# A layer's opening: the first tile's modulation weights, scale ahead of shift, and a small vector on another queue

## The chip, the cores and the metric

The kernel runs on one core of one Trainium2 chip. The metric is the device time of one execution in microseconds. A core has five engines that run side by side and are kept in step by semaphores: TensorE (PE in the profile) for matrix products, with its weight loads shown apart as PEld, VectorE (DVE), ScalarE (ACT), GpSimd (POOL) and SyncE (SP), which here does little else than issue DMA transfers. [...]

## The reference, cut to what matters

One layer over 512 latent tokens and 256 context tokens of 1024 channels. Before the first norm is used, a vector `c` (and `c_ctx` for the context) is turned into a scale and a shift for each channel:

```
mod = silu(c) @ w_mod + b_mod                # 6 x 1024 values; the same for c_ctx
sh1, sc1, gt1, sh2, sc2, gt2 = split(mod, 6)
h = rmsnorm(x, norm1_g) * (1 + sc1) + sh1    # latent; the context with its own sc1, sh1
p = h @ w_in                                 # one wide projection; its column groups feed two mixers
...
o  = merge(ssd mixer, window attention, two sigmoid gates) @ w_out
x  = x + gt1 * o
x  = x + gt2 * conv_ffn(rmsnorm(x, norm2_g) * (1 + sc2) + sh2)
return rmsnorm(x, final_g)
```

All of this is in float32. The kernel holds a float32 operand as a high part and a low part and forms a product from three matrix products: high by high, high by low, low by high.

## The kernel before, in words

Channels lie on the 128 partitions, so 1024 channels are eight tiles, j = 0 to 7, and tokens run along the free axis. The change touches only the opening stage, up to about 62 us, in which the norm's scales and shifts are computed while the first five column blocks of the projection (the gates, `w0`, 640 columns) and then one q and one k block are multiplied.

The projection does not wait for the norm's root. For tiles j = 0 to 4 the kernel multiplies `x * a1` (a1 is the channel's `(1 + scale) * norm gain`), multiplies the sums by the root later (`sc`), and adds the part that comes from the shifts as a bias, which is formed from products of the shifts with `w0` (`Z`). For tiles 5 to 7 the whole normed value is used. So per tile j the steps are, by the names that the plan gives them:

- `Lm(2j)`, `Lm(2j+1)`: two loads of modulation weights, 512 KB each (`load_mod`, L433 to L435). `Lx`: a tile of x, 256 KB. `Lw`: a tile of `w0`, 320 KB. `Lv`, once: the vectors (`vec`) and the identity (`ident`).
- `A(j).0`, `A(j).1` on PE (`mod_rows`, L474 to L479): each load holds four of the eight blocks of input channels, for 256 output columns, 128 of shift and 128 of scale. Both are needed before any value is complete. Four products go to four strips of 32 rows of the accumulator `pmod`.
- `tm(j)` on ACT (`mod_copy`, L483) copies the sums out; `B(j)` on PE (`mod_cols`, L487) adds the four strips and turns the row into a column, once for the shift and once for the scale, with a small matrix `sel2` that `tv` (`tables`, L402 to L405, DVE) makes from `ident`; `a(j)` on DVE (`mod_put`, L490 and L491) writes `a1` and `s1`.
- `hi(j)` (ACT, L503) and `lo(j)` (DVE, L507): the high and the low part of `x * a1`. `wh(j)` (ACT, L495) and `wl(j)` (DVE, L499): those of `w0`.
- `P(j).i.t` on PE (`product`, L523): for five column blocks i the three products t = 0, 1, 2 (wh with hi, wh with lo, wl with hi), 15 for a tile.
- `s(j)` (DVE, L622) and `Z(j)` on PE (`shifts`, L542): the products of the shifts with `w0`.
- `sq(j)`, `ad(j)`, and once `S`, `m`, `R`, `T`, `p`: sums of squares, root and its spread. `n(j)` and what follows: the normed value with its high and low parts.

Before the plan, `cc` (the two vectors `c`, 8 KB) is loaded into `ccs` by a DMA that ACT issues (L386). ACT and DVE turn it into silu values, laid out in `csil32` as weights of 32 columns (L393 to L397). Nine warm-ups (`warm`, L407 to L409, a product of ones with ones that nobody reads) keep PE busy meanwhile. A float32 product shows as two PE records.

The order on PE, ACT and DVE in this stage is written out at build time by a planner (`Plan`, L282 to L357). Each step, an "atom", has an engine, a cost, the steps that it needs and a rank. The planner walks through simulated time, takes for each engine the lowest rank that is ready (or the one that is ready first), and emits the steps in that order inside a `manual_schedule` block. SP's loads keep the order in which they are listed; their time comes from bytes over a common bus. The starting points are given at the call:

```
run_plan(first_.order({"ACT": 3.0, "DVE": 3.6, "SP": 0.7}, bus=2.76))
```

More warm-ups are atoms too: two after A0.0, two after A0.1, five after B0 (L601 to L603). Outside such blocks the order within an engine comes from the framework; at a few places `keep_in_program_order` binds it.

Of the kernel before, what the change touches and what calls it, by code (L numbers as in the profile page):

```python
# [13 lines left out]
ALU = mybir.AluOpType  # L14
# [4 lines left out]
P = 128  # L19
# [3 lines left out]
KT = D // P  # L23
# [4 lines left out]
V_BMOD = 0  # L28
# [16 lines left out]
def tile_hybrid_layer(  # L45
# [30 lines left out]
    nc = tc.nc  # L76
    V, S, G, T = nc.vector, nc.scalar, nc.gpsimd, nc.tensor
# [123 lines left out]
    ccs = cpool.tile([P, KT, 2], F32, name="ccs")  # L201
# [10 lines left out]
    s1 = cpool.tile([P, KT, 2], F32, name="s1")  # L212
# [11 lines left out]
    def col(base, i):  # L224
        return vec[:, base + i : base + i + 1]
# [151 lines left out]
    with tc.tile_pool(name="spool", bufs=1) as sp:  # L377
# [5 lines left out]
        sel4 = sp.tile([P, 4], F32, name="sel4")  # L383
        gb = cpool.tile([P, 8], F32, name="gb")

        S.dma_start(ccs, cc)  # L386
        G.memset(csil32, 0.0)
        G.memset(s32, 0.0)
        G.memset(phalf, -0.5)
# [19 lines left out]
            T.matmul(pg[NG - 1][:, 0:P], ones, ones, start=True, stop=True, skip_group_check=True)  # L409
# [23 lines left out]
        def load_mod(i):  # L433
            t = mod_raw[i] = sp.tile([P, 4, 256], F32, tag="wm", name="wm", bufs=6)
            nc.sync.dma_start(t, wm1[i].rearrange("p (k c) -> p k c", k=4))  # L435

        def load_w0(j):
            r = w0_raw[j] = sp.tile([P, 640], F32, tag="w0", name="w0", bufs=4)
            nc.sync.dma_start(r, w0[j])
# [17 lines left out]
            nc.sync.dma_start(ident, ident_d)  # L457

        for j in range(KT):
            for i in (2 * j, 2 * j + 1):  # L460
                load_atom("Lm%d" % i, 512, lambda i=i: load_mod(i), ["A%d.%d" % divmod(i - 6, 2)] if i > 5 else [])
# [12 lines left out]
        def mod_rows(j, u):  # L474

            w = mod_raw.pop(2 * j + u)
            for k in range(4):
                z = slice(32 * k, 32 * k + 32)
                T.matmul(pmod[z, 0:256], csil32[:, 4 * u + k, :], w[:, k, :], start=u == 0, stop=u == 1)  # L479

        def mod_copy(j):
            rows[j] = tmp("tm")[:, :256]
            S.copy(rows[j], pmod[:, 0:256])  # L483

        def mod_cols(j):
            for i in range(2):
                T.matmul(pmod[:, 256 + 2 * i : 258 + 2 * i], rows[j][:, i * P : (i + 1) * P], sel2, start=True, stop=True)  # L487

        def mod_put(j):
            V.tensor_scalar(a1[:, j, :], pmod[:, 258:260], bp1[:, j : j + 1], col(V_N1, j), ALU.add, ALU.mult)  # L490
# [28 lines left out]
        def part(ps, key, n, w, h, t):  # L519

            a, b = ((0, 0), (0, 1), (1, 0))[t]
            c = B_[key] = B_.get(key, 0) + 1
            T.matmul(ps, w[a], h[b], start=c == 1, stop=c % n == 0, skip_group_check=True)  # L523

        def product(j, i, t):
            h = (hi_[j], lo_[j]) if j < NU else (hlh[:, j, :], hll[:, j, :])

            n = 3 * NU if j < NU else 3 * KT
            part(pg[i], ("P", i), n, [w[j][:, i * P : (i + 1) * P] for w in (wh, wl)], h, t)

        def product2(n, k, t):

# [65 lines left out]
            V.tensor_scalar_mul(nsink, bcs[:, 32:48], -1.0)  # L598

        CR = 450  # L600
        for x, n in (("A0.0", 2), ("A0.1", 2), ("B0", 5)):  # L601
            for i in range(n):
                atom("W%s.%d" % (x, i), "PE", 0.23, [x], 0, warm)  # L603
        r = {}
        cq = tmp("te")[:, :LC]
        for j in range(KT):
            R, js = 100 * j, "%d" % j
            for u in range(2):
                needs = ["Lm%d" % (2 * j + u)] + (["A%d.0" % j] if u else ["tm%d" % (j - 1)] if j else [])
                atom("A%d.%d" % (j, u), "PE", 0.5, needs, R - 110 + u, lambda j=j, u=u: mod_rows(j, u))  # L610
            needs = ["A%d.1" % j] + (["B%d" % (j - 1)] if j else [])
            atom("tm" + js, "ACT", 0.37, needs, R - 108, lambda j=j: mod_copy(j))
            needs = ["tm" + js, "a%d" % (j - 1) if j else "tv"]
            atom("B" + js, "PE", 0.4, needs, R - 107, lambda j=j: mod_cols(j))
            atom("a" + js, "DVE", 0.41, ["B" + js], R - 106, lambda j=j: mod_put(j))
            old = ["P%d.%d.%d" % (j - 2, i, t) for i in range(NG) for t in range(3)] if j > 1 else []
            atom("wh" + js, "ACT", 0.72, ["Lw" + js] + old, R - 60, lambda j=j: w_high(j))
            atom("wl" + js, "DVE", 0.82, ["wh" + js] + ["a0"] * (j == 0), R - 60, lambda j=j: w_low(j))
            if j < NU:
                atom("hi" + js, "ACT", 0.72, ["a" + js, "Lx" + js] + old, R - 100, lambda j=j: x_high(j))  # L620
                atom("lo" + js, "DVE", 0.75, ["hi" + js] + old, R - 100, lambda j=j: x_low(j))
                atom("s" + js, "DVE", 0.15, ["a" + js], R - 70, lambda j=j: V.tensor_copy(s32[:, j, 0:1], s1[:, j, 0:1]))  # L622
# [1289 lines left out]
def pack(  # L1912
# [71 lines left out]
```

## Time and profile before

| | us |
|---|---|
| median of three runs | 1260.78 |
| the runs | 1264.44, 1260.48, 1260.78 |
| the profiled execution's own time | 1263.37 |
| its span, first to last instruction | 1261.6 |

The mean granted clock of TensorE in the profiled execution is 0.995 of full speed. In the profile, an L number is a line of the kernel. A row of the timeline gives start, length, engine, line, operation, out<-in, how many instructions were merged, and in brackets how long the engine had been idle before and what released it. The chain is the sequence of work that ended last, followed back from the last instruction. A DMA row gives the size and the time from issue to landing, the waiting in its queue included. Names of tiles stand without their numbers: `wm` are the modulation weights, `w` the tiles of `w0`, `ah` and `al` are hi and lo, `mis` the accumulators of the five column blocks, `acc` holds `pmod` and the bias sums.

### The profile page before, as it was taken

The page shows a single profiled execution, that of the slowest core. Times are in us where ns is not written, and L with a number is a line of the kernel's source. Part 1 is how long each engine was busy: PE and PEld are TensorE (multiplying, and loading weights), DVE is VectorE, ACT ScalarE, POOL GpSimd, SP SyncE. Part 2 cuts the span into 40 slices and gives each one's busy share as a digit, 9 for nine tenths or more (in the row PEclk, how much of TensorE's full clock was granted, in tenths as well). Part 3 has the DMA queues.
Part 4 walks back from the last instruction along what each step waited for, and adds up shares of the span by engine and source line. Part 5 has one row for each costly group of instructions (what it writes and reads, how often), then busy time and mean ns, then how long its engine had stood idle before and what let it go on. Part 6 is the DMA issues. An engine that isn't in the chain of part 4 may idle for free.

```text
span 1261.6 us, 17339 instructions
## 1 busy us (share of the span) xinstructions
PE 1245.1 (99%) x6466; PEld 1029.8 (82%) x6466; DVE 878.7 (70%) x1417; ACT 656.3 (52%) x1223; POOL 138.5 (11%) x113
## 2 busy tenths in 40 slices
PE   9999999999999999999999999999999999999997
PEld 6798888888788788787787787889988888888886
DVE  4857788888636688878988667676777777773333
ACT  4658788887344476565565653223544444442221
POOL 0000000000000143343343420000200000000000
PEclk9999999999999999999999999999999999999998
DMA  9652143212354235445347378775233333333331
GB/s 375 232 135 91 56 134 91 92 61 78 133 166 130 89 107 157 133 125 181 101 124 219 109 244 268 240 245 196 73 112 117 117 114 105 116 113 92 103 94 67
DMA packets 90996, 174.57 MB, mean 138 GB/s; under 512 B 7712, under 2 KB 43360, under 8 KB 90912
## 3 DMA queue, kind: packets, MB, share of 16 engines
q1 hardware_dynamic: 89680, 172.40, 42.9%
q8 instruction: 51, 0.84, 0.3%
q10 hardware_dynamic: 1232, 1.06, 0.2%
q14 instruction: 33, 0.27, 0.1%
HBM read 150.82 MB, written 17.11 MB: 133 GB/s over the span
## 4 chain that ended last, share of the span: by engine, by line
PE 83%; DVE 8%; ACT 2%; DMA 2%; POOL 2%; issue 1%; DVEq 0%; SPq 0%; POOLq 0%; ACTq 0%
PE acc L191 19%; PE acc L194 19%; PE acc L192 19%; PE score L884 3%; PE po L933 3%; PE mis L523 2%; PE pt L920 2%; DVE wlo L149 2%; PE mis L1507 1%; PE mis L1501 1%; PE acc L1003 1%; PE acc L1005 1%; PE acc L1004 1%; PE acc L1794 1%; PE acc L1664 1%
## 5 line engine op out<-in xcount | busy, mean ns | idle before, releaser
L149 DVE TENSOR_TENSOR wlo<-wraw,whi 128x1024 fp32r<-128x1024 f32 (+1 forms) x128 | 163.9, 1281 | 119.0 <-ACT whi L148 118.0
L148 ACT CAST whi<-wraw 128x1024 fp32r<-128x1024 f32 (+1 forms) x128 | 132.1, 1033 | 179.1 <-PE acc L192 122.8
L191 PE MATMUL acc<-hlh,whi 128*128 128x512 f32 x472 | 193.9, 411 | 0.0
L194 PE MATMUL acc<-hlh,wlo 128*128 128x512 f32 x472 | 185.1, 392 | 0.0
L192 PE MATMUL acc<-hll,whi 128*128 128x512 f32 x472 | 184.5, 391 | 0.0
L191 PE MATMUL acc<-mh,whi 128*128 128x512 f32 x368 | 143.4, 390 | 0.0
L192 PE MATMUL acc<-ml,whi 128*128 128x512 f32 x368 | 143.2, 389 | 0.0
L194 PE MATMUL acc<-mh,wlo 128*128 128x512 f32 x368 | 143.2, 389 | 0.0
L194 PEld LDWEIGHTS acc<-hlh,wlo 128*128 128x128 f32 x472 | 88.6, 188 | 19.6
L192 PEld LDWEIGHTS acc<-hll,whi 128*128 128x128 f32 x472 | 88.9, 188 | 17.5 <-issue 2.4
L191 PEld LDWEIGHTS acc<-hlh,whi 128*128 128x128 f32 x472 | 88.8, 188 | 17.0 <-issue 2.4
L194 PEld LDWEIGHTS acc<-mh,wlo 128*128 128x128 f32 x368 | 69.1, 188 | 14.4
L191 PEld LDWEIGHTS acc<-mh,whi 128*128 128x128 f32 x368 | 69.1, 188 | 14.4
L192 PEld LDWEIGHTS acc<-ml,whi 128*128 128x128 f32 x368 | 69.1, 188 | 14.2
L1415 POOL TENSOR_TENSOR st<-st,eT 128x512 f32<-128x512 f32 x24 | 29.4, 1224 | 409.0 <-ACT st L1432 389.5
L893 DVE CUSTOM_DVE_ANT_0 p<-score,winm,nsink 128x512 f32<-128x512 f32 (+1 forms) x64 | 51.9, 811 | 16.4 <-PE score L884 14.9
L191 PE MATMUL acc<-fh,whi 128*128 128x512 f32 x154 | 60.0, 390 | 0.0
L194 PE MATMUL acc<-fh,wlo 128*128 128x512 f32 x154 | 59.9, 389 | 0.0
L192 PE MATMUL acc<-fl,whi 128*128 128x512 f32 x154 | 59.9, 389 | 0.0
L245 POOL TENSOR_TENSOR rs<-ms,phalf 128x2 f32<-128x2 f32 (+1 forms) x5 | 4.8, 951 | 490.6 <-DVE ms L244 490.6
L900 ACT ACTIVATE p<-p,mneg 128x512 f32<-128x512 f32 (+1 forms) x64 | 49.7, 777 | 16.1 <-DVE mneg L893 15.6
L1314 ACT ACTIVATE ta<-acc,half 128x512 f32<-128x512 f32 (+1 forms) x66 | 46.6, 706 | 20.1 <-PE acc L194 18.9
(365 smaller groups left out, 2917.9 us busy)
## 6 DMA issues: line engine op xcount, KB each, us to landing
wraw<-wup SPq DMA_DIRECT2D x44, 512.0 KB, 3.5
fb<-cs_d SPq DMA_DIRECT2D x32, 512.0 KB, 5.8
wraw<-wm SPq DMA_DIRECT2D x32, 512.0 KB, 3.8
wraw<-wx SPq DMA_DIRECT2D x24, 512.0 KB, 3.5
wm<-wm SPq DMA_DIRECT2D x16, 512.0 KB, 8.1
wraw<-wz SPq DMA_DIRECT2D x16, 512.0 KB, 3.6
wraw<-wos SPq DMA_DIRECT2D x16, 512.0 KB, 4.9
wraw<-wdn SPq DMA_DIRECT2D x16, 512.0 KB, 3.4
```

The source lines that it names most:

```text
L148: S.copy(hi[:, :n], r[:, :n])
L149: V.tensor_tensor(lo[:, :n], r[:, :n], raw(hi[:, :n]), ALU.subtract)
L191: T.matmul(ps, wh, xh[:, k0 + k, :], start=a, stop=False)
L192: T.matmul(ps, wh, xl[:, k0 + k, :], start=False, stop=False)
L194: T.matmul(ps, wl, xh[:, k0 + k, :], start=False, stop=b)
L523: T.matmul(ps, w[a], h[b], start=c == 1, stop=c % n == 0, skip_group_check=True)
L884: T.matmul(ps[:, o : o + len(z) * P], Q[h][:, b * P : (b + 1) * P], k[:, j, z[0] * P : (z[-1] + 1) * P], start=v == 0 and o % 512 in (0, P ...
L893: V.tensor_tensor_reduce(p[:, :w], d["ps"][i][:, o0 : o0 + w], m, op0=ALU.add, op1=ALU.min, scale=1.0, scalar=nsink[:, h : h + 1], accum_o ...
L900: S.activation(p, p, AF.Exp, bias=d["mneg"][:, i : i + 1], scale=-1.0, accum_out=d["den"][:, i : i + 1])
L933: T.matmul(d["po"], vst[:, cols[x], j, :], d[y][x], start=x == 0 and y == "pth", stop=x == c - 1 and y == "ptl")
L1314: S.activation(o[:, :n], ps[:, :n], AF.Identity, scale=hcol(base_w, stride + i), bias=hcol(base_b, i))
L1415: G.tensor_tensor(h8(n), h8(s), bc64(eT[:, z0 : z0 + 8, c]), ALU.mult)
```

## The change

For the first tile (j = 0) only, the two modulation loads no longer hold four blocks of input channels each for shift and scale together. Lm0 holds all eight blocks for the 128 scale columns, Lm1 all eight for the 128 shift columns; the arrays are laid out so on the host. Lm0 stays at the head of the loads, Lm1 moves behind the first tile of `w0`. A0.0, A0.1, tm0 and B0 become two chains: A0a, tma, B0a for the scale, which `a0` needs, and A0b, tmb, B0b for the shift, which `s0` needs. A0b waits for the tile's first product P0.0.0, tmb for B0a. The shift's two DVE operations become the step `s0`. Lm6 and Lm7, which reuse the two buffers, wait for A0a and A0b.

The load of `cc` goes from ACT's queue to SP's, ahead of all other loads. The opening warm-ups become ten; the warm-ups in the plan are two after A0a and six after B0a. `wl1` now needs `a1`, `B1` needs `s0`, and the norm of a tile needs its shift. The planner's starting points are changed.

```diff
-        S.dma_start(ccs, cc)
+        nc.sync.dma_start(ccs, cc)
...
-            for _ in range(9):
+            for _ in range(10):
                 warm()
...
         for j in range(KT):
-            for i in (2 * j, 2 * j + 1):
+            for i in (2 * j, 2 * j + 1)[: 1 + (j > 0)]:
...
             load_atom("Lw%d" % j, 320, lambda j=j: load_w0(j), old)
+            if j == 0:
+                load_atom("Lm1", 512, lambda: load_mod(1))
...
+        def mod_first(u):
+            w = mod_raw.pop(u).rearrange("p k (a c) -> p (k a) c", a=2)
+            for k in range(KT):
+                z = slice(32 * (k % 4), 32 * (k % 4) + 32)
+                T.matmul(pmod[z, P - P * u : 2 * P - P * u], csil32[:, k, :], w[:, k, :], start=k < 4, stop=k > 3)
+
+        def first_copy(u):
+            rows[u, 0] = tmp("tm")[:, :P]
+            S.copy(rows[u, 0], pmod[:, P - P * u : 2 * P - P * u])
+
+        def first_cols(u):
+            T.matmul(pmod[:, 258 - 2 * u : 260 - 2 * u], rows[u, 0], sel2, start=True, stop=True)
+
+        def first_shift():
+            V.tensor_scalar(s1[:, 0, :], pmod[:, 256:258], col(V_BMOD, 0), None, ALU.add)
+            V.tensor_copy(s32[:, 0, 0:1], s1[:, 0, 0:1])
...
-            V.tensor_scalar(s1[:, j, :], pmod[:, 256:258], col(V_BMOD, j), None, ALU.add)
+            if j:
+                V.tensor_scalar(s1[:, j, :], pmod[:, 256:258], col(V_BMOD, j), None, ALU.add)
...
-        for x, n in (("A0.0", 2), ("A0.1", 2), ("B0", 5)):
+        for x, n in (("A0a", 2), ("B0a", 6)):
             for i in range(n):
-                atom("W%s.%d" % (x, i), "PE", 0.23, [x], 0, warm)
+                atom("W%s.%d" % (x, i), "PE", 0.23, [x], -1, warm)
...
+            if j == 0:
+                for u, x in enumerate("ab"):
+                    atom("A0" + x, "PE", 0.55, ["Lm%d" % u] + ["P0.0.0"] * u, R - 110 + 40 * u, lambda u=u: mod_first(u))
+                    atom("tm" + x, "ACT", 0.25, ["A0" + x] + ["B0a"] * u, R - 108 + 40 * u, lambda u=u: first_copy(u))
+                    atom("B0" + x, "PE", 0.25, ["tm" + x, "tv"], R - 107 + 40 * u, lambda u=u: first_cols(u))
...
-            atom("wl" + js, "DVE", 0.82, ["wh" + js] + ["a0"] * (j == 0), R - 60, lambda j=j: w_low(j))
+            atom("wl" + js, "DVE", 0.82, ["wh" + js] + ["a" + js] * (j < 2), R - 60, lambda j=j: w_low(j))
...
+                    atom("s0", "DVE", 0.3, ["B0b"], R - 70, first_shift)
...
-            needs = ["pl", "a" + js, "sq" + js] + (["lo" + js] if j < NU else [])
+            needs = ["pl", "a" + js, "sq" + js] + (["lo" + js, "s" + js] if j < NU else [])
...
-        run_plan(first_.order({"ACT": 3.0, "DVE": 3.6, "SP": 0.7}, bus=2.76))
+        run_plan(first_.order({"PE": 5.2, "ACT": 3.0, "DVE": 3.6, "SP": 1.2}, bus=3.2))
...
+    m0 = w_mod[:, :2048].reshape(KT, P, 2, KT, P)[:, :, ::-1, 0, :]
+    d["wm1"][0:2] = m0.transpose(2, 1, 0, 3).reshape(2, P, 1024)
```

More of the change, by code (lines that the diff above doesn't have):

```diff
@@ L459, in tile_hybrid_layer @@
         for j in range(KT):
-            for i in (2 * j, 2 * j + 1):
-                load_atom("Lm%d" % i, 512, lambda i=i: load_mod(i), ["A%d.%d" % divmod(i - 6, 2)] if i > 5 else [])
+            for i in (2 * j, 2 * j + 1)[: 1 + (j > 0)]:
+                load_atom("Lm%d" % i, 512, lambda i=i: load_mod(i), ["A%d.%d" % divmod(i - 6, 2) if i > 7 else ("A0a", "A0b")[i - 6]] if i > 5 else [])
             if j == 0:
@@ L525, in product @@
         def product(j, i, t):
-            h = (hi_[j], lo_[j]) if j < NU else (hlh[:, j, :], hll[:, j, :])
+            h = (hi_.get(j), lo_.get(j)) if j < NU else (hlh[:, j, :], hll[:, j, :])
             n = 3 * NU if j < NU else 3 * KT
-            part(pg[i], ("P", i), n, [w[j][:, i * P : (i + 1) * P] for w in (wh, wl)], h, t)
+            part(pg[i], ("P", i), n, [w[j][:, i * P : (i + 1) * P] if j in w else None for w in (wh, wl)], h, t)
         def product2(n, k, t):
@@ L607, in tile_hybrid_layer @@
             R, js = 100 * j, "%d" % j
-            for u in range(2):
-                needs = ["Lm%d" % (2 * j + u)] + (["A%d.0" % j] if u else ["tm%d" % (j - 1)] if j else [])
-                atom("A%d.%d" % (j, u), "PE", 0.5, needs, R - 110 + u, lambda j=j, u=u: mod_rows(j, u))
[L611 to L615, printed above, removed]
+            if j == 0:
[3 more added lines that the diff above has]
+                    atom("B0" + x, "PE", 0.25, ["tm" + x, "tv"], R - 107 + 40 * u, lambda u=u: first_cols(u))
+            for u in range(2 if j else 0):
+                needs = ["Lm%d" % (2 * j + u)] + (["A%d.0" % j] if u else ["tm%d" % (j - 1) if j > 1 else "tmb"])
+                atom("A%d.%d" % (j, u), "PE", 0.5, needs, R - 110 + u, lambda j=j, u=u: mod_rows(j, u))
+            if j:
+                needs = ["A%d.1" % j] + (["B%d" % (j - 1)] if j > 1 else [])
+                atom("tm" + js, "ACT", 0.37, needs, R - 108, lambda j=j: mod_copy(j))
+                needs = ["tm" + js, "a%d" % (j - 1)] + ["s0"] * (j == 1)
+                atom("B" + js, "PE", 0.4, needs, R - 107, lambda j=j: mod_cols(j))
+            atom("a" + js, "DVE", 0.41 if j else 0.25, ["B" + js] if j else ["B0a"], R - 106, lambda j=j: mod_put(j))
             old = ["P%d.%d.%d" % (j - 2, i, t) for i in range(NG) for t in range(3)] if j > 1 else []
             atom("wh" + js, "ACT", 0.72, ["Lw" + js] + old, R - 60, lambda j=j: w_high(j))
-            atom("wl" + js, "DVE", 0.82, ["wh" + js] + ["a0"] * (j == 0), R - 60, lambda j=j: w_low(j))
+            atom("wl" + js, "DVE", 0.82, ["wh" + js] + ["a" + js] * (j < 2), R - 60, lambda j=j: w_low(j))
             if j < NU:
```

5 lines of the change are left out of this document (4 added, 1 removed).

## The prediction

> **What bounds the kernel now.** I read the page first, then the chain that ended last, cut to the opening, then the opening's timeline and its DMA issues, and last a table of stages. The page:
>
> ```profile
> span 1261.6 us, 17339 instructions
> PE 1245.1 (99%) x6466; PEld 1029.8 (82%) x6466; DVE 878.7 (70%) x1417; ACT 656.3 (52%) x1223; POOL 138.5 (11%) x113
> ```
>
> TensorE (PE) is busy for 99% of the span, so a saving in the opening lasts to the end if it lets PE begin *useful* work sooner and PE then stays fed. PE's warm-up products (L409) count as busy too, so the opening has to be read by name. The pieces of the chain that ended last (start, length, what):
>
> ```profile
> 0.73 4.15 DMA ccs<-cc
> ...
> 5.64 0.19 DVE csil L397
> 5.87 0.64 PE acc L479 x8
> ...
> 7.15 0.57 PE acc L479 x8
> 8.82 1.22 PE mis L409 x10
> 10.04 0.24 PE acc L542
> 12.17 0.57 PE acc L479 x8
> 14.10 0.34 PE acc L487 x4
> 24.54 0.56 PE acc L542 x4
> ```
>
> The conditioning vector `ccs` lands at 4.88 us, ScalarE (ACT) and VectorE (DVE) turn it into `csil32` by 5.83, and only then does the first modulation product A0.0 start, at 5.87. Until 10.04 PE alternates between first-tile products and warm-ups; a warm-up is time that PE had nothing to do. The same opening on the timeline (start, length, engine, line, what):
>
> ```profile
> 1.05 3.73 PE L409 MATMUL mis<-ones 128*128 128x128 f32 x18 [1.05 <-DVE ones L392]
> 2.12 0.43 SPq L457 DMA_DIRECT2D ident<-ident_d  x1
> 2.59 0.71 SPq L442 DMA_DIRECT2D xsb<-xT  x1
> 3.34 0.43 SPq L439 DMA_DIRECT2D w<-w  x1
> 6.88 0.16 DVE L405 TENSOR_SCALAR bp<-vec 128x8 f32<-128x8 f32 x1
> 7.79 0.37 ACT L483 COPY tm<-acc 128x256 f32<-128x256 f32 x1 [2.67 <-PE acc L479]
> 8.15 0.72 ACT L495 CAST w0h<-w 128x640 fp32r<-128x640 f32 x1
> 8.21 0.61 PE L487 MATMUL acc<-sel,tm 128*128 128x2 f32 x4
> 8.92 0.28 DVE L490 TENSOR_SCALAR a<-acc,bp,vec 128x2 f32<-128x2 f32 x1 [1.88 <-ACT w0h L495]
> 9.23 0.72 ACT L503 ACTIVATE ah<-xsb,a 128x512 fp32r<-128x512 f32 x1 [0.35 <-DVE a L490]
> 9.86 0.61 ACT L549 ACTIVATE ssq<-xsb 128x512 f32<-128x512 f32 x1
> 9.97 0.41 PE L542 MATMUL acc<-w,s 128*32 128x256 f32 x3
> 10.96 0.50 PE L523 MATMUL mis<-ah,w0h 128*128 128x512 f32 x1
> ```
>
> From 9.97 us PE does only useful work: Z0 and A1.0 woven together (9.97 to 10.96), then the first tile's products P0. That point, 9.97, is what the change has to beat. And two rows of the stage table (length, then busy time of each engine, granted clock, DMA share, GB/s):
>
> ```profile
> 10.00:40.00 30.00, 30.00 (x216) 19.82 (x216) 17.89 (x41) 16.48 (x34) 1.47 (x1) 1.00 1.03 411
> 40.00:62.00 22.00, 22.00 (x128) 17.01 (x127) 21.37 (x42) 13.99 (x27) 1.61 (x1) 1.00 0.50 176
> ```
>
> PE is without a gap in both stretches; DMA is full to 40 us, DVE nearly full (21.37 of 22) behind it. PE ends last, with two neighbours close by.
>
> **The change, part by part.** Landings come from the DMA issues of the first 5 us (KB each, then median us from issue to landing), one row for the first `wm` load alone, and small stores from the whole run:
>
> ```profile
> wm<-wm SPq DMA_DIRECT2D x4, 512.0 KB, 5.2
> ident<-ident_d SPq DMA_DIRECT2D x1, 64.0 KB, 4.6
> xsb<-xT SPq DMA_DIRECT2D x1, 256.0 KB, 4.7
> w<-w SPq DMA_DIRECT2D x1, 320.0 KB, 4.8
> ccs<-cc ACTq DMA_DIRECT2D x1, 8.0 KB, 4.2
> ```
> ```profile
> DMA to landing us min/median/max: 4.0/4.0/4.0
> ```
> ```profile
> tt_d<-tt SPq DMA_DIRECT2D x2, 0.4 KB, 2.7
> tt_d<-tt SPq DMA_DIRECT2D x2, 0.1 KB, 1.9
> ```
>
> *1. `cc` goes first on SP's queue.* It moves from ACT's queue, where it was issued at 0.73, to SP's, ahead of every other load. Every SP load is therefore issued one slot later; the slot is about 0.45 us (from `ident` at 2.12 to `xsb` at 2.59 is 0.47). For `cc` nothing stands in front any more. Its landing is bounded from below by the small stores (1.9 and 2.7 us after issue) and from above by today's 4.2. I take 2.7, the nearest in size at the head of a queue: 0.74 + 2.7 = 3.4, and with the 0.99 from landing to A0 (4.88 to 5.87) `csil32` stands at 4.4. ACT saves the issue, which is hidden under its wait for `cc` anyway.
>
> *2. The first load becomes scale only, and the shift load goes behind `w0`.* Lm0 is issued at 0.74 + 0.45 = 1.19 and lands 4.0 later, at 5.2 (today 4.7). The lower end is 4.7, if the delayed start is made up; I keep 5.2. Between Lm0 and `ident`, `x0`, `w0` stand 512 KB less, which at the 411 GB/s of the stage table is 1.28 us. Today they land at 2.12 + 4.6 = 6.7, 2.59 + 4.7 = 7.3, 3.34 + 4.8 = 8.1. After: 0.45 later and 1.28 sooner, so 5.9, 6.5 and 7.3. Lm1 (shift) takes the slot after `w0`, and lands at 8.1 + 0.45 = 8.6, as the bytes up to there are today's. All later loads are 0.45 late.
>
> *3. The tenth opening warm-up* adds two of PE's records behind the eighteen that end at 4.78. Ten in 1.22 us are 0.12 each, so it ends at about 5.0, under the wait for Lm0. Costs nothing; if Lm0 came at 4.7, it would cost 0.3.
>
> *4. The short chain to the first scale.* A0a starts at 5.2: eight products of 128 columns where A0.0 has four of 256, so the same 0.64 us, to 5.85. The copy is 128 columns wide, not 256: bounded by 0.37 and half of it, I take 0.25, so 6.2 with the 0.07 hand-over (7.72 to 7.79). The tables need `ident` at 5.9 and today end 0.34 after its landing (6.7 to 7.04), so 6.2: a tie, and B0a starts at 6.25. B0 to the scale is 8.92 - 8.21 = 0.71 with four records; two fewer at 0.11 leaves 0.49, so `a0` starts at 6.75. `hi0` follows 0.31 later (8.92 to 9.23), at 7.05, where `x0` (6.5) is there. `wh0` needs `w0` at 7.3. The two share ACT, 0.72 each at a pitch of 0.63 (9.23 to 9.86), and the first product needs both: `hi0` first gives 8.4, `wh0` first 8.65. Which one the planner puts first hangs on hundredths of its costs; I take the middle, **8.5**. Against 9.97 that is 1.45 us sooner.
>
> *5. What was hidden comes into the open.* The shift half of the first tile, once under the wait, now stands between useful products. A0b: 0.57 (the piece at 12.17) and a changeover of about 0.1. B0b: half of the 0.34 piece, and 0.1: 0.27. Z0 has to wait for the shift and so loses A1.0's company: alone it is 0.56, and A1 alone 0.57, together 1.13 against 0.99 today, with 0.1 for the changeover: 0.24. In all 0.67 + 0.27 + 0.24 = 1.18. A0b waits for Lm1 at 8.6, about when the first product is in; if it is late, P0's other products run first, since ten of the fifteen need only `wh0`, `hi0` and `lo0`.
>
> *6. Extra and moved small work.* One more ACT copy (0.25), `s1` and its copy moved into an operation of their own on DVE, `wl1` after `a1`, the norms after the shifts: ACT has 16.48 busy of 30 us and DVE 17.89, and between 10 and 40 us PE waits for neither. Nothing, so long as that holds. The doubled waits put A1.0 behind the second copy; P0 then still has most of its fifteen products to cover that.
>
> *7. The six warm-ups behind B0a* instead of five run until about 7.8 and end before 8.5. Nothing.
>
> **Sum:** 1.45 - 1.18 = about **0.25 us faster**. The profiled execution had span 1261.6 and own time 1263.37; it would become about 1261.35 and 1263.1. The median of the runs shown is 1260.78, 2.6 below the profiled one, so the forecast is 1260.5. Ends of this mechanism: with Lm0 at 4.7, `hi0` first and Z0 still woven in, the first product comes at 8.25 (the warm-ups hold A0a to 5.0) and 0.94 stays behind it: 0.8 faster. With `wh0` first and Lm1 0.3 late: 0.2 slower.
>
> [...]
>
> **The rivals.**
>
> *Rival 1: `cc` is no faster at the head of SP's queue.* If it keeps its 4.2 us, `csil32` stands at 5.9 and A0a starts 0.67 later than I take it, and so does `hi0`, at 7.7. With `wh0` from 7.3 ahead of it the first product comes at 8.65, with `wh0` behind it at 9.05; the middle, 8.85, leaves 1.12 - 1.18, so 0.1 slower: 1260.9. For it: 4.2 is the only price of this load. Against: the small stores' 1.9 and 2.7. It decides from a landing of 4.2 us on.
>
> *Rival 2, the other side: the clock.* The opening eighteen take 0.207 us each and later ones 0.12, so PE begins at half its clock. If the full clock comes later than A0a's start, or is lost in the pause between the last warm-up (7.8) and 8.5, the first products run at half pace. The trace has such a stretch after PE idled:
>
> ```profile
> PE acc L191 <- ACT whi L148: 1.8, 1, 1.8
> 745.00:772.00 27.00, 25.18 (x108) 19.70 (x107) 17.95 (x25) 13.50 (x20) 1.02 (x1) 0.94 0.86 281
> ```
>
> A mean of 0.94 over 27 us is 3.3 us at half clock, so 1.6 us of PE's work lost. The price here is the same: 1.6 - 0.25, so 1.4 slower, 1262.1. Against it: the opening is denser than before, as the pause ahead of A0 shrinks from 1.1 us to 0.2. [...]
>
> *Rival 3: the rest of the kernel moves.* The order is written by hand only inside the `manual_schedule` blocks; elsewhere the framework orders ACT, DVE, GpSimd and SP, and a different opening can give it a different order. The trace of before can't show whether it does. The bound is what PE now idles for others between 90 us and the end: the groups of PE's waits
>
> ```profile
> PE mis L1342 <- DVE tc L1323: 2.1, 3, 0.8
> PE mis L251 <- POOL rs L245: 1.3, 1, 1.3
> PE mis L234 <- ACT tc L1678: 1.3, 1, 1.3
> PE score L884 <- ACT te L840: 0.7, 1, 0.7
> ```
>
> and the 1.8 above, 7.2 us together. Doubled or gone, they give 1267.7 or 1253.3; a worse order is likelier than a better one, since PE is idle so little that there is more to lose than to win.
>
> *Rival 4: the gain is eaten later.* PE starts sooner but DVE, 21.37 of 22 us busy from 40 to 62, or the loads, 0.45 later, end where they did. Then the time is unchanged or up to 0.45 slower: 1260.8 to 1261.2. For it stands the DVE figure of that row, against it that PE has no gap in either row of the stage table, so that it, and neither of the two, ends last there now.
>
> **How the numbers follow.** A measurement of this kernel tells about 0.3%, 3.8 us, from no change: above 1264.6 or below 1257.0. My mechanism has 0.45 (1260.0 to 1261.0), rival 1 0.08, rival 2 0.12, rival 4 0.11, all within; rival 3 has 0.24, of which I put 0.14 beyond 1264.6 and 0.09 below 1257.0. So faster 0.09, same 0.77, slower 0.14. The range that leaves out no more than two in ten takes in rivals 1, 2 and 4 and the near part of rival 3, with the spread of the three runs (1260.48 to 1264.44): 1258.3 to 1265.5.
>
> **What would show it.** `ccs` landing near 3.4 and not 4.9; A0a at 5.2; `ident`, `x0`, `w0` at 5.9, 6.5 and 7.3; the first L523 product at 8.5, then an A group and a lone B and Z group between products; P1 beginning only a few tenths sooner than today; 40 to 62 us as it was, a little sooner. The forecast is wrong if A0a still waits for `csil32`, if the granted clock is low after 5 us, if PE has gaps between 9 and 40 us, or if the stages after 62 us differ in length: then rival 3 holds.

## The result, and the profile after

| | median us | lowest to highest | runs |
|---|---|---|---|
| kernel before | 1261.74 | 1260.48 to 1264.44 | 7 |
| changed kernel | 1266.16 | 1264.49 to 1269.32 | 7 |

The ratio is 1.0035, with an interval of 1.0024 to 1.0045: some 4.4 us slower, where 0.25 us faster was forecast. The profiled execution's own time is 1269.32, its mean granted clock 0.994. The first two lines of its page:

```profile
span 1267.5 us, 17376 instructions
PE 1248.3 (98%) x6482; PEld 1029.9 (81%) x6482; DVE 877.7 (69%) x1417; ACT 655.6 (52%) x1224; POOL 139.7 (11%) x113
```

The span grew by 5.9 us: PE is busy for 3.2 us more than before, and idle for 2.7 us more. The chain that ended last, cut to the opening (start, length, what):

```profile
3.07 5.62 DMA w<-w
8.71 0.02 ACT w0h L516
9.34 0.73 ACT ah L524
10.11 0.51 PE mis L544
10.61 0.57 PE acc L488 x16
11.19 1.58 PE mis L544 x3
12.77 0.22 PE acc L495 x2
12.98 1.01 PE acc L481 x8
```

The modulation vector no longer heads this chain; the load of `w0` does. It was issued at 3.07 (3.34 before), and landed at 8.69. From there the high part of `w0` and then `ah` (hi0) lead to the first useful product at 10.11. Before, useful work began at 9.97. The last rows show a second thing: an A group of eight takes 1.01 us (L481), where the same group took 0.57 before. The timeline of the same opening shows what stood idle (start, length, engine, line, and in brackets the idle time before it):

```profile
2.48 0.22 ACT L393 ACTIVATE csil<-ccs 128x16 f32<-128x16 f32 x1 [0.47 <-DMA ccs<-cc]
5.00 0.65 PE L488 MATMUL acc<-wm,csil 128*32 128x128 f32 x16
6.28 1.58 PE L409 MATMUL mis<-ones 128*128 128x128 f32 x12
6.46 0.28 DVE L510 TENSOR_SCALAR a<-acc,bp,vec 128x2 f32<-128x2 f32 x1 [0.56 <-PE acc L495]
8.71 0.72 ACT L516 CAST w0h<-w 128x640 fp32r<-128x640 f32 x1 [2.73 <-DMA w<-w]
9.34 0.72 ACT L524 ACTIVATE ah<-xsb,a 128x512 fp32r<-128x512 f32 x1
10.11 0.51 PE L544 MATMUL mis<-ah,w0h 128*128 128x512 f32 x1 [2.25 <-ACT ah L524]
```

The short chain to the first scale works better than forecast: `ccs` is in at 2.46, A0a runs from 5.00, the scale is ready at 6.74. Then it is of no use: ACT waits 2.73 us for `w0`, with hi0 behind it in the written order, and PE, its warm-ups over at 7.86, stands still for 2.25 us. The table by stage (length, busy time of PE, PEld, DVE, ACT and POOL, granted clock, DMA share, GB/s):

```profile
10.00:40.00 30.00, 29.89 (x203) 18.14 (x207) 14.50 (x35) 13.43 (x27) 0.00 (x0) 0.89 1.03 410
40.00:62.00 22.00, 22.00 (x138) 16.27 (x131) 19.84 (x37) 12.58 (x26) 3.08 (x2) 1.00 0.33 120
```
```profile
12.00:13.00 1.00, 1.00 (x8) 0.79 (x11) 0.00 (x0) 0.00 (x0) 0.00 (x0) 0.50 1.03 421
```

From 10 to 40 us the mean granted clock is 0.89, and it is 0.50 in the microsecond from 12. The records put the half clock at 11.1 to 17.9 us, 6.8 us in which PE did half its work: 3.4 us lost. At the end of the stage (the same PE instruction in both) this execution is 4.88 us behind: 0.14 from the later start, 3.4 from the clock, which leaves 1.3 for work that used to be hidden.

### The profile page after: what moved, and what is told of

The parts are those of the page before. It is cut to its first block, busy times and chain, and to the rows that moved or that the text cites. A ratio compares the mean times of both kernels' runs of the same rounds, so it can differ in the third digit from the quotient of the medians.

```text
span 1267.5 us, 17376 instructions
## 1 busy us (share of the span) xinstructions
PE 1248.3 (98%) x6482; PEld 1029.9 (81%) x6482; DVE 877.7 (69%) x1417; ACT 655.6 (52%) x1224; POOL 139.7 (11%) x113
## 3 DMA queue, kind: packets, MB, share of 16 engines
q10 hardware_dynamic: 1088, 1.05, 0.2%
## 4 chain that ended last, share of the span: by engine, by line
PE 79%; DVE 9%; DMA 4%; ACT 2%; POOL 2%; issue 2%; SPq 0%; DVEq 0%; ACTq 0%; POOLq 0%
PE acc L191 18%; PE acc L192 18%; PE acc L194 17%; PE score L915 3%; PE po L964 3%; PE mis L544 3%; PE pt L951 2%; DVE wlo L149 2%; PE mis L1538 1%; DMA wraw<-wm 1%; PE mis L1532 1%; PE acc L1034 1%; PE acc L1036 1%; PE acc L1035 1%; PE acc L1825 1%
## 5 line engine op out<-in xcount | busy, mean ns | idle before, releaser
L1346 DVE SCALAR_TENSOR_TENSOR ta<-acc,half,ta 128x511 f32<-128x511 f32 (+1 forms) x66 | 43.8, 663 | 19.5 <-ACT ta L1345 19.5
```

The costliest lines, as they stand in the source:

```text
L1346: V.scalar_tensor_tensor(o[:, 1:n], ps[:, 0 : n - 1], hcol(base_w, i), o[:, 1:n], ALU.mult, ALU.add)
```

## The experiments

Three explanations were open after this profile, and a run could have any mix of them: the clock falls to half in the new pause; `w0` lands late and hi0 waits behind it; and the shift half of the first tile, once hidden, costs PE more than the 1.18 us of the forecast. A fourth part, `cc` on SP's queue, could help or harm by itself. In the kernels that add or drop warm-ups only products that nobody reads are added or dropped; no kernel leaves out a part of the computation. Ratios are to the kernel before on the same chip, with a 95% interval; 0.001 is 1.26 us.

**The changed kernel again, unaltered.**

> The changed kernel unaltered, beside the experiments on the same chip. Theory C (the clock): PE's pause between the last warm-up (7.9 us) and the first product (10.1) closes the clock gate, so this run shows half clock in the stretch 10 to 18 us and is 0.2 to 0.4% slower than before. Theory E (exposure): the shift half of the first tile standing between useful products costs about 1.2 us and the late first product 0.1, 0.1% in all, whatever the clock. Theory N (the loads): w0's first tile lands at about 8.7 in this run too, 1.4 us later than its bytes would have it; if it was chance it lands near 7.3.

Measured: 1263.87, ratio 1.0018 (1.0008 to 1.0028). Its chain, cut to the opening:

```profile
3.07 4.73 DMA w<-w
...
8.45 0.72 ACT ah L524
9.18 0.04 issue
9.22 0.50 PE mis L544
9.72 0.57 PE acc L488 x16
10.29 0.90 PE mis L544 x3
11.19 0.12 PE acc L495 x2
11.31 0.57 PE acc L481 x8
...
13.11 0.42 PE acc L563 x4
...
19.19 0.56 PE acc L563 x4
```

Here the same load landed 0.9 us sooner, at 7.79, the warm-ups filled the wait, and the clock stayed full (1.00 in each stretch from 10 to 62 us): an A group is back at 0.57. So the half clock belongs to some executions and not to the change as such, and the kernel is slower without it. The chain also shows the exposed work by name: A0b (9.72), B0b (11.19), A1.0 alone (11.31), Z0 alone (13.11) and Z1 alone (19.19), all of which stood between warm-ups or woven into another group before. How long PE needs from its first useful product to the first of the q and k blocks' low-part products is the measure of it. That marker in the timeline of before, and then of this run:

```profile
57.37 0.62 PE L523 MATMUL acc<-hlh,wlo 128*128 128x512 f32 x2
```
```profile
58.55 0.62 PE L544 MATMUL acc<-hlh,wlo 128*128 128x512 f32 x2
```

Before it is 57.37 - 9.97 = 47.40, here 58.55 - 9.22 = 49.33. One more q product (0.23) stands ahead of the marker here, so the exposed work is 1.70 us. Added up from the pieces of the two chains by line: A and Z groups 0.85 more, B groups 0.31, and 0.54 for the same 75 products of tiles 0 to 4, which are cut up more often.

**More warm-ups, so that PE has no pause.**

```diff
-                atom("W%s.%d" % (x, i), "PE", 0.23, [x], -1, warm)
+                more = 9 if (x, i) == ("B0a", 5) else 1
+                atom("W%s.%d" % (x, i), "PE", 0.23, [x], -1, lambda more=more: [warm() for _ in range(more)])
```

> The changed kernel with eight more warm-ups (16 PE records, about 1.8 us) behind the last one after B0a, so that PE is kept busy to about 9.7 us. Nothing else moves. Theory C: full clock through 10 to 18 us, 3.0 to 3.4 us less than the changed kernel, so 0.1% slower than before or level with it. Theory E alone: no difference from the changed kernel.

Measured: 1264.37, ratio 1.0025 (1.0016 to 1.0035). The chain of its opening:

```profile
6.83 3.23 PE mis L409 x28
10.06 0.24 PE mis L544
```

The clock never fell, in the profile (1.00 in each stretch from 10 to 62 us) or in the ten runs (mean clock 0.997 or 0.998 in all). Yet the kernel is no faster than the unaltered one. In this profile `w0` landed at 8.14, which by the 1.42 us from landing to product of the other profiles allows a first product at about 9.55; the 28 warm-up records stand before it in the chain, and by the timeline it began at 9.81. So part of what they save is paid back at once. The clock is not the main part of the loss.

**`cc` back on ACT's queue.**

```diff
-        nc.sync.dma_start(ccs, cc)
+        S.dma_start(ccs, cc)
```

> The changed kernel with the load of cc back on ACT's queue; the rest as changed. If the move of cc pays, A0a starts at about 5.9 here instead of 5.0, and the first product no later than in the changed kernel, since it waits for w0. If the move is what makes w0 late (theory N by the cc load), w0 lands near 7.0 here. Theory C: the pause of PE is shorter by about 0.9 us, so the gate closes less often; 0 to 3.4 us less than the changed kernel. Theory E alone: as the changed kernel.

Measured: 1262.22, ratio 1.0012 (1.0002 to 1.0022). From the DMA issues of its first 5 us (KB each, median us from issue to landing), and then the same rows of the changed kernel's first profile:

```profile
w<-w SPq DMA_DIRECT2D x1, 320.0 KB, 4.4
...
ccs<-cc ACTq DMA_DIRECT2D x1, 8.0 KB, 3.8
```
```profile
w<-w SPq DMA_DIRECT2D x1, 320.0 KB, 5.6
...
ccs<-cc SPq DMA_DIRECT2D x1, 8.0 KB, 1.7
```

At the head of SP's queue `cc` takes 1.7 us and not 3.8, and that is worth nothing here, since A0a waits for Lm0 (4.78) and for the warm-ups. With `cc` on ACT every SP load starts one slot sooner, `w0` lands at 7.01, and the first product comes at 8.86. Of the three changed kernels run on this chip it has the lowest ratio, though its interval overlaps that of the unaltered one.

**The kernel before with only `cc` moved to SP,** run on two chips.

```diff
-        S.dma_start(ccs, cc)
+        nc.sync.dma_start(ccs, cc)
```

> The kernel before with only the load of cc moved to SP's queue, ahead of the rest. csil32 is ready before the first load of weights lands, so A0.0 starts at about 5.1 instead of 5.9, A0.1 when Lm1 lands at about 6.4, the first scale at about 8.2 instead of 8.9; w0 lands at about 8.5, and wh0 and hi0 share ACT, so useful work begins within 0.3 us of before. Theory C: PE's pauses are under 1.3 us, the clock holds. All: within 0.1% of before.

> The kernel before with only the load of cc at the head of SP's queue, once more. First time 0.9994 (0.9985 to 1.0003). If csil32 by 3.4 us instead of 5.8 lets the first products start 0.3 to 0.5 us sooner, 0.9994 to 0.9998 again; if the first result was chance, 1.000.

Measured: 1260.39, ratio 0.9994 (0.9985 to 1.0003), and 1262.53, 0.9997 (0.9986 to 1.0008). A0.0 starts at 5.20 and no longer at 5.87, useful work at 9.53, but both intervals hold 1. The move neither makes nor loses a measurable amount alone.

**The new layout with everything else as before:** `cc` on ACT, nine warm-ups, both loads at the head, the old starting points; once with A0b free to run in the wait, once with A0b behind the first product as in the change.

```diff
-            for i in (2 * j, 2 * j + 1)[: 1 + (j > 0)]:
+            for i in (2 * j, 2 * j + 1):
...
-            if j == 0:
-                load_atom("Lm1", 512, lambda: load_mod(1))
...
-                    atom("A0" + x, "PE", 0.55, ["Lm%d" % u] + ["P0.0.0"] * u, R - 110 + 40 * u, lambda u=u: mod_first(u))
+                    atom("A0" + x, "PE", 0.55, ["Lm%d" % u], R - 110 + 40 * u, lambda u=u: mod_first(u))
```

(This is against the changed kernel. The last pair of lines stands in the first of the two only; the lines for `cc`, the warm-ups and the starting points are not shown.)

> Of the change only the layout and the two short chains: cc on ACT's queue, nine opening warm-ups, both first loads at the head as before, and A0b no longer waits for the first product, so the shift half is done under the wait for w0. Theory E (exposure): what the change lost was the shift half and Z0 standing between useful products, so here PE's stretch from its first useful work to its first q or k product with a low weight is again 47.4 us (49.3 in the changed kernel) and the time is that of before, 0.9995 to 1.0005. A theory that blames the layout or the split chains themselves: 1.001 or more.

> As the run beside it (layout alone), but A0b waits for the first product again. The loads come as in before, so w0 is on time (8.1) and PE's pauses are short. Theory E: PE's stretch is 49.1 to 49.3 us, the first product comes at about 9.1 (useful work began at 9.97 before), together 0.8 to 1.1 us slower than the layout alone, ratio to before 1.0006 to 1.001. If the whole loss of the changed kernel came from late loads or a closed clock gate, this one is level with before.

Measured: hidden 1263.31, ratio 1.0013 (1.0004 to 1.0022); exposed 1263.30, 1.0007 (0.9998 to 1.0016). If exposed work were all there is, the first would stand level with before and the second would be 0.8 to 1.1 us slower than the first. The second's ratio lies where it was forecast, though its interval holds 1; but the first is not level with before, and the two medians are the same. The chain of the first shows part of the reason:

```profile
8.71 0.78 PE mis L409 x6
9.49 0.56 PE acc L561 x4
10.04 0.44 PE mis L542
10.48 0.57 PE acc L479 x8
...
18.64 0.56 PE acc L561 x4
```

Useful work began at 9.42, 0.55 sooner than in the first profile of before. But Z0 (0.56 from 9.49) and Z1 (18.64) stand alone here as well, where before the four and the eight instructions of Z and A ran woven together (10.04 to 11.03, 0.99 for both). The stretch from first useful work to the marker is 48.36 and not 47.40. The planner's new order of the whole stage, and not only the hidden shift half, eats the earlier start. How much each takes can be counted to one and the same PE instruction at the end of the stage (its rows stand further below). From the first useful work to it, two later profiles of before need 49.13 us, the first kernel here 50.17, the second 50.91, and the changed kernel 50.92. So of these 1.8 us (1.70 by the marker in the first profile of before), 1.0 comes with the new order while the shift half is still hidden, and 0.75 with A0b and B0b in the open.

**`w0` loaded ahead of the first tile of x.**

```diff
+            if j == 0:
+                load_atom("Lw0", 320, lambda: load_w0(0))
             for k in XS.get(j, ()):
                 load_atom("Lx%d" % k, 256, lambda k=k: load_x(k))
...
-            load_atom("Lw%d" % j, 320, lambda j=j: load_w0(j), old)
+            if j:
+                load_atom("Lw%d" % j, 320, lambda j=j: load_w0(j), old)
```

> The changed kernel with the first w0 tile loaded ahead of the first x tile, so that wh0 is done while x0 is on its way. If the first product waits for w0's landing and then for two ACT operations in a row (9.2 to 10.1 us in the two profiles of the changed kernel), it comes about 0.6 us sooner here, at 0.75 us behind the later of x0's landing and a0's end, and the time falls by 0.6 us against the changed kernel. If it waits for the scale chain, nothing changes.

Measured: 1264.27, ratio 1.0018 (1.0009 to 1.0027). Now `w0` is in at 6.95 and x at 7.87, and the wait for x replaces the wait for `w0`; the first product comes at 8.73, half a microsecond sooner than in the profile of the unaltered kernel above, and the ratio is the same. The weight loads of A0b then waited 0.37 us for Lm1, until 9.63, and the PE instruction at the stage's end came at 60.14, as in that profile (60.15). The late load alone is not the loss either.

**The kernel before with `cc` on SP and the vectors ahead of the second modulation load.**

```diff
-            if j == 0:
-                load_atom("Lv", 200, load_vec)
+                if i == 0:
+                    load_atom("Lv", 200, load_vec)
```

> The kernel before with the load of cc at the head of SP's queue and the vectors and the identity ahead of the second modulation load: the parts that brought something, without the split. A0.0 at about 5.1, tables done by 6.3, A0.1 at 7.0, scale by 8.6; w0 at 8.6 to 8.9 then sets the first product, as in the run with cc alone moved. 0.9985 to 1.0000 of before.

Measured: 1265.04, ratio 1.0023 (1.0013 to 1.0034), the slowest of its set. Its timeline, and a row of its stages:

```profile
8.53 1.08 PE L479 MATMUL acc<-wm,csil 128*32 128x256 f32 x8 [2.06 <-DMA wm<-wm]
```
```profile
10.00:15.00 5.00, 5.00 (x32) 4.23 (x31) 2.69 (x6) 2.57 (x5) 0.00 (x0) 0.50 1.03 415
```

A0.1 waited until 8.53 for its load, where 7.0 was forecast, PE paused for 2.06 us, and the granted clock was a half from 8.6 to 15.4. This is the kernel before but for two places in the load order, so the clock can fall to half without the split. It is not this kernel's main loss: three of its nine runs have a mean clock of 0.996 or less, and the other six still average 1264.9, 2.9 us above before.

**The changed kernel without the six warm-ups behind B0a,** the opposite of the second run.

```diff
-        for x, n in (("A0a", 2), ("B0a", 6)):
+        for x, n in (("A0a", 2), ("B0a", 0)):
```

> The changed kernel without the six warm-ups behind B0a; every other instruction in its order. PE then pauses from about 6.4 us to the first product at 9.2 to 10.1, 2.8 to 3.7 us instead of 1.4 to 2.3. Theory C (the clock): the gate closes in most runs (mean granted clock 0.996 or less; 3 of 17 runs of the changed kernel did so, none of 62 of the kernel before), each time at 1.7 to 3.4 us, so the median is 1.5 to 3.5 us above the changed kernel's on this chip. If the pause doesn't matter, it is level with the changed kernel.

Measured: 1265.51, ratio 1.0031 (1.0018 to 1.0044). Timeline and stage row:

```profile
8.86 0.80 PE L544 MATMUL mis<-ah,w0h 128*128 128x512 f32 x1 [2.13 <-ACT ah L524]
```
```profile
10.00:15.00 5.00, 5.00 (x38) 2.61 (x31) 0.97 (x3) 0.89 (x2) 0.00 (x0) 0.50 1.03 408
```

With the pause made certain, eight of ten runs have a mean clock of 0.996 or less; those eight average 1266.4, the other two 1263.3. Where a run lost its clock is seen in the profiled ones only, here from 8.4 to 15.2 us. The mean clock tells it only roughly: the first profiles of before and of the changed kernel also end with 8.1 and 7.2 us at half clock, which alone gives a mean of 0.997, other runs have 0.998, and a stretch of 3.4 us at half clock takes 0.0014 off, so a short one can hide in 0.997. The counts are lower bounds. Across all sets of the unaltered changed kernel four of 23 runs had so low a mean clock, of the ten with more warm-ups none, and of 96 timed runs of the kernel before none. (The 0.995 of the profiled execution before is the stretch near 762 us that the prediction quotes.) In each set the runs with a low clock lie some two to three and a half microseconds above the others in the mean; at 3.4 us and 4 of 23 that is 0.6 us a run. The forecast difference between the kernels does not show: 1.0031 lies within the 1.0018 to 1.0035 that the unaltered changed kernel has in its sets.

**More profiles of both kernels,** two of before and two of the changed one.

> The kernel before, unaltered, for a second profile of it. If the first was a fair sample, A0.0 starts at 5.9, useful work begins at about 10.0, and the products of the stage at 60.1 us there come within 0.3 us of that; the half-clock stretch at 762 us, 1.7 us of it, may be missing. If the opening of before varies as that of the changed kernel does (first product 8.7 to 10.1), it shows by 0.5 us and more.

> As the run beside it, a third profile of the kernel before: opening within 0.3 us of the first, w0 landed at 8.1 to 8.5.

> The changed kernel, unaltered, for a third profile. w0 at 7.8 to 8.7 (theory N: always late by 0.5 to 1.4 us against its bytes, 7.3), first product 1.4 us behind it, the stage's end 1.0 us later than in before, and 1.7 to 3.4 us more if the clock gate closes in the pause.

> The changed kernel unaltered, on the same chip. From the trace: stage 1.0 us late, and 1 run in 6 with a closed gate, 3 us: 1.5 us in the mean, ratio 1.0012 if L1 and nothing else; 1.002 to 1.0035 as measured so far.

Measured: before 1261.45 and 1261.03; changed 1264.38, and with more runs 1266.44, ratio 1.0033 (1.0020 to 1.0045). In the four profiles of the changed kernel `w0` landed at 8.69, 7.79, 7.58 and 7.35, and the first product came 1.42 or 1.43 later each time (10.11, 9.22, 9.00, 8.78): the rule of this opening is load, wh0, hi0, product. In the three of before useful work began at 9.97, 10.09 and 9.47. The last two profiles of before and the three of the changed kernel without a half clock in the opening can be set side by side:

| us | before | changed | difference |
|---|---|---|---|
| first useful work on PE | 9.78 | 9.00 | -0.78 |
| end of the stage (the same PE instruction) | 58.91 | 59.92 | +1.01 |
| end of PE's last instruction | 1253.54 | 1256.65 | +3.11 |
| from the second row to the third | 1194.63 | 1196.73 | +2.10 |
| PE idle from 66 to 1248 us | 5.52 | 6.78 | +1.26 |
| span | 1259.46 | 1262.54 | +3.08 |

The instruction at the end of the stage and PE's last ones, first in one profile of before and then in one of the changed kernel:

```profile
59.22 0.39 PE L523 MATMUL acc<-hll,whi 128*128 128x512 f32 x1
...
1252.75 1.12 PE L251 MATMUL mis<-ident,rs 128*128 128x128 f32 x4 [1.31 <-POOL rs L245]
```
```profile
59.92 0.39 PE L544 MATMUL acc<-hll,whi 128*128 128x512 f32 x1
...
1255.67 1.12 PE L251 MATMUL mis<-ident,rs 128*128 128x128 f32 x4 [1.29 <-POOL rs L245]
```

The idle time is from the stage tables of the same two (length, then PE's busy time):

```profile
66.00:1248.00 1182.00, 1176.37 (x6034) 979.53 (x6033) 827.62 (x1302) 617.44 (x1150) 132.46 (x99) 1.00 0.42 129
```
```profile
66.00:1248.00 1182.00, 1175.26 (x6012) 977.02 (x6012) 827.95 (x1303) 618.00 (x1151) 131.42 (x98) 1.00 0.42 129
```

So 1.0 of the 3.1 us arises in the stage, and 2.1, two thirds, behind it. Of these 2.1, PE idles for 1.26, and for the remaining 0.8 it counts as busy. Followed instruction by instruction, PE's lag stays as it was from 62 to 365 us and again from 815 us to the end; it changes between 365 and 390, 500 and 600, and 700 and 815 us, and in these places single executions of one kernel differ by up to a microsecond and more as well. The order of the engines there is the same in both kernels but for one exchange on DVE near 68 us: the `wlo` of a weight block now stands ahead of the last addition of the first rotated block (`tb`). The runs speak against that exchange as the cause. The two layout-only kernels and the one with `w0` first lack it, and idle 6.94, 7.25 and 6.74 us there; the one with more warm-ups and the one with `cc` on ACT have it, and idle 6.28 and 6.20. PE's waits show where (what PE waited for, us, times, longest), of before and then of the changed kernel:

```profile
PE mis L1342 <- DVE tc L1323: 1.9, 4, 0.7
...
PE mis L1430 <- DVE xw L1401: 0.5, 1, 0.5
PE mis L1413 <- DVE xw L1401: 0.5, 1, 0.5
```
```profile
PE mis L1373 <- DVE tc L1354: 2.4, 3, 1.1
PE mis L1444 <- DVE xw L1432: 1.0, 2, 0.7
...
PE mis L1461 <- DVE xw L1432: 0.5, 1, 0.5
```

These are handovers from DVE that already waited before; in this pair of profiles two are half a microsecond longer and one is the same. Among the rows not shown, the wait for `wlo` is shorter (1.4 before, 0.2 after) and waits of 0.5 each for `whi` and `yl` are new, so no single wait makes the difference. What makes the stretch longer was not found.

**Useful work of the kernel before put off by warm-ups,** 1.1 us and 3.1 us ahead of Z0.

```diff
-                atom("W%s.%d" % (x, i), "PE", 0.23, [x], 0, warm)
+                more = 6 if (x, i) == ("B0", 4) else 1
+                atom("W%s.%d" % (x, i), "PE", 0.23, [x], 0, lambda more=more: [warm() for _ in range(more)])
```

(15 in place of 6 for the longer one.)

> The kernel before with five more warm-ups (ten PE records at 0.11 us) ahead of Z0, so that all useful work on PE begins 1.1 us later and nothing else changes. Theory L1 (a delay is passed on one to one): 1.1 us slower, ratio 1.0009. Theory L2 (it grows in the later stages): 2 us and more, ratio 1.0016 or more.

> As the run beside it with fourteen more warm-ups: 3.1 us. L1: ratio 1.0025. L2: 5 to 6 us, 1.0040 to 1.0048. If some of the delay is made up by the loads that are ahead by then: less than 3.1 us, under 1.002.

Measured: 1262.61, ratio 1.0007 (0.9997 to 1.0016), so 0.9 us for 1.1; and 1266.24, 1.0034 (1.0021 to 1.0048), so 4.3 (2.6 to 6.0) for 3.1. A microsecond lost in the opening costs about one at the end, perhaps 1.4; the interval of the longer one holds both. The two profiles, one of each, put the end of the stage 0.9 and 3.3 us later than in before, and from there to the end of PE's last instruction they need 1194.80 and 1196.19 us, where before needs 1194.63. So a delay of 0.9 us did not make the rest longer, while one of 3.3 us went with 1.6 more. At about the smaller delay the changed kernel has 2.1 more, in each of its three profiles between 1.8 and 2.3. As far as one profile can show, its late stage alone does not explain that.

## Why the prediction was wrong, by its steps

1. *`cc` first on SP.* Right in kind, and the load was faster than taken: `ccs` at 2.46 and not 3.4. Rival 1 falls with it: the traces show 1.7 us at the head of SP's queue and 3.7 to 4.2 on ACT's. The runs don't separate the queue from the 0.45 us by which `cc` now goes ahead of the 512 KB load. But nothing waits for `cc` any more, and alone the move measures 0.9994 and 0.9997.

2. *The loads.* Lm0 came at 4.78 (5.2 forecast), but `w0` at 8.69 where 7.3 was forecast, and at 7.35 to 7.79 in the other three profiles. **This is the first step that failed.** It also counted one slot too many: as Lm1 moves back, `ident` and the first tile of x are issued at 2.12 and 2.59 as before, so its own working gives 6.8 for `w0` and not 7.3. It took the 411 GB/s of a later stage for the first microseconds. The stage tables of after show 342 to 360 GB/s from 4 to 7 us, in those three microseconds together 0.18 MB less than 411 would bring, or 0.4 us. The rest is not a matter of the rate: in the profile of the changed kernel with the lowest one, 335 GB/s, `w0` came at 7.58. The spread of 1.3 us between executions of one kernel was not thought of, and what makes it is open.

3. *The tenth warm-up.* Free, as forecast, though not for the reason given: in the second profile the twenty records of these warm-ups took 4.64 us, to 5.69, and not 4.03, and held A0a to 5.62, which itself took 1.08 us and not 0.65. The late `w0` hid that.

4. *The first product at 8.5.* The scale was early (6.74), and the tie on ACT fell on the side named as the worse: wh0 first in every profile. With it hi0, which could have run from 6.74, waits for `w0`. The step's rule, `w0` and the two ACT steps behind it, held (1.42 measured, 1.35 from 7.3 to 8.65); its input was late by 0.05 to 1.4. Of the 1.45 us sooner, 0.78 remained in the executions with a full clock, and none in the first one.

5. *The exposed work.* **The second that failed**, by size: 1.70 us and not 1.18. The lone A0b, B0b and Z0 were in the sum. Z1, which also lost its company, and the products cut up more often (0.54) were not. The layout-only kernels split it: A0b and B0b cost 0.75 where 0.94 was forecast, and the new order 1.0 where 0.24 was. The step priced the pieces that move, and not the new order that the planner writes around them.

6. *Small work.* Right as far as the stage goes: PE is busy for 29.89 of the 30 us from 10 to 40, and for all of the 22 behind.

7. *"Nothing" for the six warm-ups.* **The third that failed**, and rival 2 in its place. In the first profile they end at 7.86, as forecast, but 2.25 us ahead of the product and not 0.7. The clock was then a half for 6.8 us, twice the stretch that the rival had priced: 3.4 us lost and not 1.6. It happens in about one run of six at least, not in every one: in the other three profiles the warm-ups lasted until 8.26 to 9.13, and the pause was 0.74 us or none. In the profiles that lost the clock in the opening PE paused for 2.06 to 2.25 us; how long a pause has to be for it was not shown.

8. *The sum.* **The fourth that failed, and the largest.** It has no term for what lies behind 62 us, on the reading that a saving in the opening lasts to the end; the rest of the kernel was left to rival 3, with a chance of 0.24. Of the 3.1 us in executions with a full clock, 2.1 arise there.

Rival 3 was right about the place, and its sign (stages of another length after 62 us) came true. Its mechanism was wrong, as the order there is the same but for one exchange that the runs speak against as the cause, and PE's idle time grew by 1.26 us and did not double. Rival 4 fails: within the stage the earlier start was spent on exposed work, and neither DVE nor the loads ended last in it.

The account that remains: per execution 1.0 us at the stage's end, 0.6 for the half clock in the mean and 2.1 behind the stage make 3.7, against 4.4, 2.3 and 4.2 us (ratios 1.0035, 1.0018 and 1.0033). The first is shown by the runs. The second rests on counts of a mean clock. That the stretch behind the stage is longer is measured, but its cause is open. No version that was run is clearly faster than the kernel before.

## What to carry to other kernels

A shorter chain to one operand is worth only what the *other* operand of the first useful product allows: forecast both landings, each with its spread between executions (1.3 us for one load here). Before a half of a step is moved out of a wait, count what it was hidden beside and what ran woven with it, since PE, 98% busy, paid for the pieces that came into the open (0.75 us for A0b and B0b here). Where a pause goes with a slower clock, as those of 2.06 to 2.25 us did here, a filler in front of a wait must outlast the late case of that wait and not its mean; take several profiles of the same kernel to learn how late it can be. And compare two kernels at the end of the changed stage as well as at the end of the run: here two thirds of the loss arose where nothing had been changed by hand.

## What the runs showed of the hardware that was not expected

- Pauses of PE of 2.06, 2.13 and 2.25 us in an opening each went with a half clock of 6.8 us (8.6 to 15.4, 8.4 to 15.2, 11.1 to 17.9 us), and one of 1.77 us near 760 us, in the first profile of before, with one of 3.4 us (761.9 to 765.3). One of 1.4 us, in the first profile of the changed kernel (PE waiting for `tc`), did not: its clock was full from 17.9 to 1260 us.
- The same twenty opening warm-up records, begun at 1.05 us in three executions of the changed kernel, took different times: A0a, right behind them, started at 5.00, 5.62 and 5.68 us.
- The same 320 KB load, issued at the same 3.07 us of the same kernel, landed between 7.35 and 8.69 us in four executions.
- PE's idle time in the 1182 us behind an opening of 60 us differed between 4.6 and 8.0 us among kernels whose order there is the same but for that one exchange.
